# A decoder layer with a 16384-expert lookup on one core: a 4 KB descriptor ring with one more place in five buffers, the h2 copy on VectorE, and outside picks found with bit masks

## The chip, the cores and the metric

The kernel runs on one core of a Trainium2 chip, as one program. TensorE multiplies, VectorE, ScalarE and GpSimd compute, and SP, ScalarE and GpSimd issue transfers. The metric is the device time of one execution in microseconds, as the median of several runs. The profile comes from one more execution, and all its times are counted from the start of its span.

## The reference

One layer works on 512 prompt tokens and 64 sample tokens of width 2048: adaLN modulation, an input projection into a gated linear recurrence and a short convolution, an output projection, a second norm and modulation (its result is called h2), then the expert layer and a last norm. The expert layer is what matters here. For every token and each of 8 heads, two sets of 128 keys are scored, the 16 best of each are combined, and the 16 best of those pairs pick experts out of 128 x 128; an expert is a row `u` of 2048 numbers and a row `v` of 2048.

```python
def peer(h, w_q, sub_keys, expert_u, expert_v):
    ...
        q = (xb @ w_q).reshape(PEER_BLOCK, PEER_HEADS, 2, HALF_DIM)
        sc = jnp.einsum('thpk,pnk->thpn', q, sub_keys).astype(jnp.float32)
        v1, i1 = lax.top_k(sc[:, :, 0], PEER_TOPK)
        v2, i2 = lax.top_k(sc[:, :, 1], PEER_TOPK)
        cand = (v1[..., :, None] + v2[..., None, :]).reshape(PEER_BLOCK, PEER_HEADS, PEER_TOPK * PEER_TOPK)
        cidx = (i1[..., :, None] * N_KEYS + i2[..., None, :]).reshape(PEER_BLOCK, PEER_HEADS, PEER_TOPK * PEER_TOPK)
        top, pos = lax.top_k(cand, PEER_TOPK)
        eidx = jnp.take_along_axis(cidx, pos, axis=-1)
        g = jax.nn.softmax(top, axis=-1).astype(xb.dtype)
        act = jax.nn.gelu(jnp.einsum('td,thkd->thk', xb, expert_u[eidx])) * g
        return jnp.einsum('thk,thkd->td', act, expert_v[eidx])
```

## The kernel before

**The stages.** Phase 1 (to about 1200 us) computes the modulation, the projections, the recurrence, the second norm and the queries. The weights `w_ada` of the modulation are streamed by SP in pieces of 1 MB (`wa`, line 185) into a pool of three buffers, `adap`; the same buffers later carry h2 to memory.

Every matmul of the expert layer is split in three: a float32 operand is rounded on ScalarE (`xhi`, line 904), the rest is taken on GpSimd (`xlo`, line 905), and TensorE adds high times high, high times low and low times high. A raw block travels as `raw` (by SP), then `xhi` and `xlo`, then 24 matmuls. Half a block of 128 experts is the unit `n` of the loop, called a half block here.

**Dense and gathered experts.** The first key of an expert names its block. The 80 blocks that are picked most (L = 80, ranked in `perm`) are computed densely for the 512 prompt tokens: the *U stage* (lines 1373 to 1377) makes the products with all `u` of a block and stores `act`; the *V stage* (line 1393) sums `v` with the weights. What prompt tokens pick from the other 48 blocks, and all picks of the sample tokens, is gathered row by row: GpSimd fetches a row for each of 128 tokens by an indirect transfer of up to 1 MB (line 1203), VectorE multiplies it with the h2 row in PSUM (`dot`, line 1231), and in the second half adds weighted `v` rows up (`add`, line 1258). There are six groups of tokens, the sample tokens and five groups of sorted prompt tokens, with 228 uses of `u` rows and h2 rows and 223 of `v` rows. Each prompt group first fetches its own h2 rows (`fetch_h`) and copies them to PSUM (`use_h`, line 1218).

**Row places.** A row needs one of RB places in the U stage and of RV in the V stage. `gather_to` fetches RB - 1 rows ahead of the use in the U stage, RV - 2 in the V stage.

**Choosing and sorting.** The last head's choice, the softmax and the sort (`choice`, `count`, `sort`) run on VectorE during the first half blocks. `count` marks the outside picks: each of the 512 picks of a partition is compared with each of the 48 outside blocks (lines 1062 to 1064). R1 is the half block in which this generator ends, R2 the one in which `all_slots` ends (the rows of each group are laid out). A generator yields an estimate of VectorE's work in microseconds; the loop adds a fixed credit for each half block (`PIECE`, `PIECE_G`) and goes on with a generator only while credit is left.

**One-hot pairs.** From R1 on, the weight of each dense expert and token is built from one-hot matrices: `g_pair` (line 1559, VectorE) makes two of them for 8 tokens, `g_scale` (line 1567, ScalarE) scales one, `g_mm` (line 1573, TensorE) multiplies them into one PSUM bank, and `g_out` (line 1580, ScalarE) copies that to `stg`. `gm` counts how far each step has come; a pair is scaled one half block after it is made and multiplied LAG half blocks after it is due.

**What sets the order.** In phase 1 a scheduler orders most engines; from the last query head on, each engine runs its instructions in the order of the code. So a late instruction holds all that stands behind it on its engine: an `hT` copy on ScalarE holds `stg`, a row product on VectorE holds `op` and `acc` (line 1415, the sum that frees a PSUM bank for TensorE).

**V stage.** Raw blocks go round four places (two in `ws`, one in `wx`, one in `vx`), loaded seven half-block units ahead (`ahead(n + 7, n + 3)`). Weights (`gsb`, `actr`) are loaded by ScalarE's queue, multiplied (`weigh`, line 1336) and halved (`halve`, lines 1343 and 1347).

Of the kernel before, what the change touches and what calls it, by code (L numbers as in the profile page):

```python
# [5 lines left out]
F32 = mybir.dt.float32  # L6
F32R = mybir.dt.float32r
I32 = mybir.dt.int32
U32 = mybir.dt.uint32
# [28 lines left out]
NCH = NA // TC  # L38
QT = NA // 128
SORTED = ((0, 64, 34), (64, 128, 47), (192, 128, 37), (320, 128, 30), (448, 64, 11))  # L40
RB = 4
RV = 6
ENDS = 5
LATE = 1
PIECE = 5.5
# [2 lines left out]
PIECE_G = 6.9  # L48
HEADS_COUNTED = 4
FULL_ROWS = 1.25  # L50
LAG = 3
FIRST_G = 6
PAIRS = 6
EARLY_V = 16
KEPT = 5
PARTS = 2
# [24 lines left out]
def build(ctx, tc, A, O, dbg=None):  # L81
# [76 lines left out]
    p1 = ExitStack()  # L158
    c1 = p1.enter_context(tc.tile_pool(name="c1", bufs=1))
    big = p1.enter_context(tc.tile_pool(name="big", bufs=1))  # L160
    adap = p1.enter_context(tc.tile_pool(name="adap", bufs=3))
    wk = p1.enter_context(tc.tile_pool(name="wk", bufs=1))
    p1p = ExitStack()
    pp = p1p.enter_context(tc.tile_pool(name="pp", bufs=2, space=PSUM))
# [477 lines left out]
    def pbank(tag, nm, bufs):  # L642
        return psum["p"].tile([128, 512], F32, name=nm, tag=tag, bufs=bufs)
# [236 lines left out]
    def load(n):  # L880
        if n >= len(stream):
            return
        s = stream[n]
        k = n % 3 if n < NU2 + 2 else (n - NU2 - 2) % 4
        pool, b = (ws, 2) if k < 2 else (wx, 1) if k == 2 else (pools["vx"], 1)
        raw = pool.tile([128, 8, 128], F32, name=f"raw{n}", tag="wraw", bufs=b)
        if s[0] == "U":
            nc.sync.dma_start(raw, A["ut"][bass.ds(block(s[1]), 1), :, 8 * s[2]:8 * s[2] + 8, :].rearrange("o p k c -> p (o k) c"))
        else:
            _, i, q = s  # L890
            r2 = raw.rearrange("p (a k) c -> p a (k c)", a=2)
            for a in range(2):
                nc.sync.dma_start(r2[:, a, :], v3[bass.ds(block(i + a), 1), :, q * VC:(q + 1) * VC].rearrange("o p c -> p (o c)"))
        raws[n] = raw
# [159 lines left out]
    def count():  # L1054

        m = nd["m"] = rt.tile([128, 3, QT], F32, name="nd_m")
        fc = rq.tile([128, 2, NA], F32, name="flags", tag="oh", bufs=2)
        fl, code = fc[:, 0, :], fc[:, 1, :]
        i1, i2 = pbank("g", "i1", 2), iselP[:, 1, :]
        S.activation(i1, iselP[:, 0, :], AF.Copy)  # L1060
        yield None
        V.tensor_scalar(fl, i1, perm[:, L:L + 1], None, op0=ALU.is_equal)
        for x in range(L + 1, 128):
            V.scalar_tensor_tensor(fl, i1, perm[:, x:x + 1], fl, op0=ALU.is_equal, op1=ALU.add)
            if x % 8 == 7:
                yield 5.0
        V.scalar_tensor_tensor(code, i1, 128.0, i2, op0=ALU.mult, op1=ALU.add)
        V.scalar_tensor_tensor(code, code, 1.0, fl, op0=ALU.add, op1=ALU.mult)
        V.tensor_reduce(m[:, 0, :], fl.rearrange("p (z k) -> p z k", k=NPK), axis=AX.X, op=ALU.add)
        for z in range(QT):  # L1070
            V.tensor_scalar(m[:, 1, z:z + 1], rowi, float(128 * z), None, op0=ALU.add)
        V.scalar_tensor_tensor(m[:, 2, :], m[:, 0, :], float(NA), m[:, 1, :], op0=ALU.mult, op1=ALU.add)
        yield 5.0
        yield None
        for z in range(QT):
            G.dma_start(pickd[z * 128:(z + 1) * 128, 0:NPK], code[:, z * NPK:(z + 1) * NPK])
            G.dma_start(pickd[z * 128:(z + 1) * 128, NPK:], topv[z].rearrange("p h k -> p (h k)"))
        for _ in range(2):
            yield None
# [126 lines left out]
    def gather_u(i):  # L1206
        p0, n, c = GT[i]
        held, st = {}, {}

        def fetch_h():  # L1210
            held["h"] = new_row(f"h2r{i}")
            G.indirect_dma_start(out=held["h"][0], out_offset=None, in_=h2d,
                                 in_offset=bass.IndirectOffsetOnAxis(ap=tok[:, i:i + 1], axis=0))

        def use_h():
            st["h"] = psum["h"].tile([128, D], F32, name=f"hT{i}", tag="hT", bufs=1)
            r, a = held.pop("h")
            S.activation(st["h"], r, AF.Copy)
            row_log[a] = True

        def fetch(j):
            held[j] = new_row(f"u{i}_{j}")
            take(held[j][0], A["u"], rows_i[i][:, j:j + 1])

        def dot(j):
            if j == 0:
                st.setdefault("h", first_h["h"])
                dots[i] = actp.tile([128, c], F32, name=f"dots{i}", bufs=1)
            r, a = held.pop(j)
            row_log[a] = True  # L1230
            V.scalar_tensor_tensor(r, r, 1.0, st["h"], op0=ALU.mult, op1=ALU.mult, accum_out=dots[i][:, j:j + 1])  # L1231

        if i:
            fetches.append(fetch_h)
            uses.append(use_h)
        for j in range(c):
            fetches.append(lambda j=j: fetch(j))
            uses.append(lambda j=j: dot(j))
# [356 lines left out]
    since = None  # L1595
    spare, due_g = -BEHIND, 0.0
    R1 = R2 = None
    gm = [0, 0, 0, 0]
    ep = None

    def upto(n):
# [9 lines left out]
    for n in range(NU2):  # L1611
# [7 lines left out]
        if R1 is not None:  # L1619
# [8 lines left out]
            while gm[2] < gm[3]:  # L1628
                g_scale(gm[2])
                gm[2] += 1  # L1630
            gm[3] = gm[0]

        even, waits = R2 is not None, False
        while spare > 0 and R2 is None:
# [87 lines left out]
    for m in range(M):  # L1722
        gi, q, bl, first, final = steps[m]
        n = NU2 + 2 * m
        ahead(n + 3, n + 3)
        ahead(n + 7, n + 3)
        if m == last:
            gather_to(NT)
        if m == last + 1:
# [179 lines left out]
```

## Time and profile before

| | |
|---|---|
| median of 3 runs | 3271.31 us (3267.7 to 3271.77) |
| the profiled execution | 3275.15 us |
| its span | 3273.3 us |
| TensorE busy in the span | 3088.6 us, 94% |
| VectorE busy | 2173.3 us, 66% |
| ScalarE busy | 1056.9 us, 32% |
| GpSimd busy | 1718.4 us, 52% |
| mean granted TensorE clock | 0.976 |
| moved by DMA | 882.84 MB, mean 270 GB/s |

Busy shares are means over stages with different limits. Rows of groups read: line, engine, operation, output from inputs, shapes and count, then busy microseconds and mean nanoseconds of one, then the idle time of the engine just before them and what ended it. A wait row reads: who waited, for whom, total microseconds, how often, the longest. In a timeline a row starts with its start and its duration, and the bracket at its end is the idle time before it.

### The profile page before, as it was taken

Reading aid. Unit: us, or ns where it says so; the run is one execution under the profiler, and the core shown is the slowest. Engines: PE = TensorE matmul, PEld = TensorE weight load, DVE = VectorE, ACT = ScalarE, POOL = GpSimd, SP = SyncE. Lnnn points to the kernel's source line nnn. Section 1 sums busy time; section 2 is a strip of 40 time slices with the busy share of each in tenths; the row PEclk is TensorE's granted clock in tenths of the full one; section 3 lists DMA queues with packets and bytes.
Section 4 is the critical chain, followed back from the end, with each engine's and each line's share of the span. In section 5 each row is a group of like instructions: output and inputs, shape, how many; then the busy total and the mean of one; then the engine's idle time right before and its main releaser. Section 6 shows DMA issues by size and latency. Waiting matters only on the chain.

```text
span 3273.3 us, 46692 instructions
## 1 busy us (share of the span) xinstructions
PE 3088.6 (94%) x17239; PEld 2616.8 (80%) x17239; DVE 2173.3 (66%) x3265; ACT 1056.9 (32%) x1645; POOL 1718.4 (52%) x1000
## 2 busy tenths in 40 slices
PE   5999999999989999999999998998999999989897
PEld 2788898889979998887788787886888777777686
DVE  3465521142246898897998979856777787978755
ACT  3244311132232222222665555542222121122122
POOL 2233233344343335666556655656777676777742
PEclk9999999999989999999999999998999999999998
DMA  9744466634342228989779898989999988998964
GB/s 375 266 144 136 163 221 203 214 99 146 131 140 67 72 90 277 308 310 381 312 297 405 340 369 315 395 285 385 389 372 387 391 327 315 344 365 305 369 218 163
DMA packets 297067, 882.84 MB, mean 270 GB/s; under 512 B 37590, under 2 KB 79446, under 8 KB 245366
## 3 DMA queue, kind: packets, MB, share of 16 engines
q1 hardware_dynamic: 160608, 380.39, 33.3%
q0 software_dynamic: 66336, 413.41, 32.1%
q10 hardware_dynamic: 69888, 86.00, 7.5%
q8 instruction: 136, 2.23, 0.3%
q14 instruction: 99, 0.81, 0.1%
HBM read 879.89 MB, written 66.81 MB: 289 GB/s over the span
## 4 chain that ended last, share of the span: by engine, by line
PE 67%; DMA 15%; DVE 7%; issue 4%; POOL 4%; ACT 2%; ACTq 0%; SPq 0%; POOLq 0%; DVEq 0%
PE pu L1373 19%; PE pv L1393 14%; PE pp_o L139 6%; DMA v<-v,rows 4%; DMA gsb<-gd 4%; PE pp_c L139 3%; PE pp_s L139 3%; PE qa L139 3%; PE pp_b L139 3%; PE qb L139 3%; PE gbank L1573 2%; PE pp_x L139 2%; PE pp_y L139 2%; PE ada L189 2%; POOL xlo L905 2%
## 5 line engine op out<-in xcount | busy, mean ns | idle before, releaser
L905 POOL TENSOR_TENSOR xlo<-raw,xhi 128x1024 fp32r<-128x1024 f32 x320 | 785.6, 2467 | 453.8 <-ACT xhi L904 440.5
L904 ACT ACTIVATE xhi<-raw 128x1024 fp32r<-128x1024 f32 x320 | 338.2, 1060 | 868.6 <-PE pv L1393 353.6
L1258 DVE SCALAR_TENSOR_TENSOR accB<-v,dots,accB 128x2048 f32<-128x2048 f32 x211 | 496.3, 2352 | 159.4 <-DMA v<-v,rows 154.0
L1231 DVE SCALAR_TENSOR_TENSOR u<-u,hT 128x2048 f32<-128x2048 f32 x223 | 505.0, 2282 | 145.1 <-DMA u<-u,rows 130.2
L1393 PE MATMUL pv<-ahi,xhi 128*128 128x512 f32 x1280 | 514.8, 402 | 43.7 <-DVE acc L1415 33.7
L1393 PE MATMUL pv<-ahi,xlo 128*128 128x512 f32 x1280 | 510.8, 399 | 10.7 <-POOL xlo L905 10.5
L1373 PE MATMUL pu<-hhi,xhi 128*128 128x512 f32 x1280 | 516.9, 404 | 1.6 <-ACT xhi L904 1.6
L1373 PE MATMUL pu<-hhi,xlo 128*128 128x512 f32 x1280 | 504.7, 394 | 6.5 <-POOL xlo L905 6.5
L1393 PE MATMUL pv<-alo,xhi 128*128 128x512 f32 x1280 | 507.7, 397 | 0.0
L1373 PE MATMUL pu<-hlo,xhi 128*128 128x512 f32 x1280 | 506.0, 395 | 0.0
L1203 POOL DMA_INDIRECT u<-u,rows x223 | 227.6, 1021 | 207.1 <-DVE u L1231 155.2
L1393 PEld LDWEIGHTS pv<-ahi,xhi 128*128 128x128 f32 x1280 | 244.3, 191 | 107.8 <-DVE acc L1415 24.8
L1393 PEld LDWEIGHTS pv<-ahi,xlo 128*128 128x128 f32 x1280 | 244.1, 191 | 72.1 <-POOL xlo L905 15.1
L1203 POOL DMA_INDIRECT v<-v,rows x223 | 260.4, 1168 | 77.9 <-issue 36.3
L1373 PEld LDWEIGHTS pu<-hhi,xlo 128*128 128x128 f32 x1280 | 242.7, 190 | 61.7 <-POOL xlo L905 7.4
L1393 PEld LDWEIGHTS pv<-alo,xhi 128*128 128x128 f32 x1280 | 244.6, 191 | 54.7
L1373 PEld LDWEIGHTS pu<-hhi,xhi 128*128 128x128 f32 x1280 | 243.3, 190 | 52.5 <-ACT xhi L904 2.1
L1373 PEld LDWEIGHTS pu<-hlo,xhi 128*128 128x128 f32 x1280 | 243.0, 190 | 47.8
L1567 ACT ACTIVATE op<-op,it 128x128 f32<-128x128 f32 x512 | 155.9, 389 | 82.5 <-DVE op L1559 82.5
L1573 PEld LDWEIGHTS gbank<-wr,op 128*128 128x128 f32 x1024 | 134.4, 193 | 42.5 <-ACT stg L1580 33.1
L1573 PE MATMUL gbank<-wr,op 128*128 128x80 f32 x1024 | 133.6, 274 | 25.7 <-ACT stg L1580 25.5
L128 POOL TENSOR_TENSOR wlo_q<-raw_q,whi_q 128x1024 fp32r<-128x1024 f32 x28 | 67.8, 2420 | 142.5 <-ACT whi_q L126 142.5
(481 smaller groups left out, 5452.2 us busy)
## 6 DMA issues: line engine op xcount, KB each, us to landing
wa<-w_ada SPq DMA_DIRECT2D x96, 1024.0 KB
raw<-ut SPq DMA_DIRECT2D x160, 512.0 KB
raw<-v SPq DMA_DIRECT2D x320, 256.0 KB
actd<-act ACTq DMA_DIRECT2D x80, 256.0 KB
gd<-stg ACTq DMA_DIRECT2D x64, 320.0 KB
gsb<-gd ACTq DMA_DIRECT2D x80, 256.0 KB
actr<-actd ACTq DMA_DIRECT2D x40, 512.0 KB
raw_o<-w_out SPq DMA_DIRECT2D x32, 512.0 KB
```

The costliest lines, as they stand in the source:

```text
L128: lo_engine(share).tensor_sub(lo, raw, r32(hi))
L139: PE.matmul(o, st, mv[pick](k), start=first, stop=last)
L189: PE.matmul(acc[32 * g:32 * g + 32, :], cpad[:, 4 * kq + g, :], w[:, g, :], start=kq == 0, stop=kq == 3)
L904: S.activation(hi, raw, AF.Copy)
L905: G.tensor_sub(lo, raw, r32(hi))
L1203: G.indirect_dma_start(out=out, out_offset=None, in_=src, in_offset=bass.IndirectOffsetOnAxis(ap=idx, axis=0), bounds_check=NE * 128 - 1, ...
L1231: V.scalar_tensor_tensor(r, r, 1.0, st["h"], op0=ALU.mult, op1=ALU.mult, accum_out=dots[i][:, j:j + 1])
L1258: V.scalar_tensor_tensor(st["a"], r, dots[i][:, j:j + 1], st["a"], op0=ALU.mult, op1=ALU.add)
L1373: PE.matmul(pu, st[:, kk, :], movA[mv](k), start=k == 0 and a == 0, stop=k == KD - 1 and a == 2)
L1393: PE.matmul(pv, st, mv, start=first and j == 0 and a == 0, stop=last and not end and j == SG - 1 and a == 2)
L1567: S.activation(ops[:, j0 + j, :], ops[:, j0 + j, :], AF.Copy, scale=it[2][:, b * 4 + j:b * 4 + j + 1])
L1573: PE.matmul(pg[:, j * L:(j + 1) * L], ops[:, j0 + j, :], wr[:, j0 + j, :], start=True, stop=True)
```

## The change

Six edits go together. The software descriptor ring, an SBUF area in which GpSimd writes the descriptors of its transfers, is set to 4096 bytes for each partition, in place of the default. With the space, five buffers get one more place: rows in the U stage (RB 5) and in the V stage (RV 7), `w_ada` pieces (4), raw V blocks (a fifth place, in `vx`, loaded eight units ahead), and one-hot pairs (PAIRS 8, four buffers in place of three). LAG is 4, and `gm` has a fifth entry, so that a pair is scaled two half blocks after it is made. `use_h` copies the h2 row to PSUM on VectorE. And `count` builds, for each partition, eight words of 16 bits from the 48 outside blocks, selects the word of each pick by eight comparisons, and shifts the pick's bit out of it; it yields 17 us of estimates in place of 30.

```diff
-RB = 4
-RV = 6
+RB = 5
+RV = 7
...
-LAG = 3
+LAG = 4
...
-PAIRS = 6
+PAIRS = 8
...
-    adap = p1.enter_context(tc.tile_pool(name="adap", bufs=3))
+    adap = p1.enter_context(tc.tile_pool(name="adap", bufs=4))
...
-        k = n % 3 if n < NU2 + 2 else (n - NU2 - 2) % 4
-        pool, b = (ws, 2) if k < 2 else (wx, 1) if k == 2 else (pools["vx"], 1)
+        k = n % 3 if n < NU2 + 2 else (n - NU2 - 2) % 5
+        pool, b = (ws, 2) if k < 2 else (wx, 1) if k == 2 else (pools["vx"], 2)
...
+        wb = rq.tile([128, 2, NA], U32, name="words", tag="oh", bufs=2)
+        word, bit = wb[:, 0, :], wb[:, 1, :]
...
+        V.memset(ki[:, 0, :], 1)
+        V.tensor_copy(ki[:, 1, :], perm[:, L:])
+        V.tensor_scalar(ki[:, 2, :], ki[:, 1, :], 15, None, op0=ALU.bitwise_and)
+        V.tensor_tensor(ki[:, 0, :], ki[:, 0, :], ki[:, 2, :], op=ALU.logical_shift_left)
+        V.tensor_scalar(ki[:, 1, :], ki[:, 1, :], 4, None, op0=ALU.logical_shift_right)
+        V.tensor_copy(kf, ki[:, 0:2, :])
+        kt = rq.tile([128, NX_], F32, name="kt", tag="v", bufs=2)
+        for w in range(8):
+            V.scalar_tensor_tensor(kt, kf[:, 1, :], float(w), kf[:, 0, :], op0=ALU.is_equal, op1=ALU.mult,
+                                   accum_out=mk[:, w:w + 1])
+        yield 4.0
         yield None
-        V.tensor_scalar(fl, i1, perm[:, L:L + 1], None, op0=ALU.is_equal)
-        for x in range(L + 1, 128):
-            V.scalar_tensor_tensor(fl, i1, perm[:, x:x + 1], fl, op0=ALU.is_equal, op1=ALU.add)
-            if x % 8 == 7:
-                yield 5.0
+        V.tensor_copy(bit, i1)
+        V.tensor_scalar(word, bit, 4, None, op0=ALU.logical_shift_right)
+        V.tensor_copy(code, word)
+        V.tensor_scalar(bit, bit, 15, None, op0=ALU.bitwise_and)
+        V.tensor_scalar(fl, code, 0.0, mk[:, 0:1], op0=ALU.is_equal, op1=ALU.mult)
+        yield 2.5
+        for w in range(1, 8):
+            V.tensor_scalar(word.bitcast(F32), code, float(w), mk[:, w:w + 1], op0=ALU.is_equal, op1=ALU.mult)
+            V.tensor_add(fl, fl, word.bitcast(F32))
+            if w == 4:
+                yield 4.5
+        V.tensor_copy(word, fl)
+        V.tensor_tensor(word, word, bit, op=ALU.logical_shift_right)
+        V.tensor_scalar(word, word, 1, None, op0=ALU.bitwise_and)
+        V.tensor_copy(fl, word)
+        yield 6.0
...
-            S.activation(st["h"], r, AF.Copy)
+            V.tensor_copy(st["h"], r)
...
-    gm = [0, 0, 0, 0]
+    gm = [0, 0, 0, 0, 0]
...
-            gm[3] = gm[0]
+            gm[3], gm[4] = gm[4], gm[0]
...
-        ahead(n + 7, n + 3)
+        ahead(n + 8, n + 3)
...
-    nc = _bacc.Bacc("TRN2", target_bir_lowering=False, num_devices=1)
+    nc = _bacc.Bacc("TRN2", target_bir_lowering=False, num_devices=1, dynamic_dma_scratch_size=4096)
```

On VectorE, where `count` marks the picks, before (`perm` holds the ranked blocks, `hT` the h2 row in PSUM, `u_27` a gathered row):

```order
L1062 TENSOR_SCALAR flags<-i_12948,perm 128x512
L1064 SCALAR_TENSOR_TENSOR flags<-i_12948,perm,flags 128x512 x15
L1231 SCALAR_TENSOR_TENSOR u_27_12891,dots_11710<-u_27_12891,hT_11373 128x2048
L1231 SCALAR_TENSOR_TENSOR u_28_12950,dots_11710<-u_28_12950,hT_11373 128x2048
L1064 SCALAR_TENSOR_TENSOR flags<-i_12948,perm,flags 128x512 x8
```

The same place with the change (`mk` holds the eight words):

```order
L1075 SCALAR_TENSOR_TENSOR kt,mk<-kf 128x48 x8
L1259 SCALAR_TENSOR_TENSOR u_26_12811,dots_11716<-u_26_12811,hT_11375 128x2048
L1259 SCALAR_TENSOR_TENSOR u_27_12852,dots_11716<-u_27_12852,hT_11375 128x2048
L1079 CAST words<-i_12955 128x512
L1080 TENSOR_SCALAR words<-words 128x512
L1081 CAST flags<-words 128x512
L1082 TENSOR_SCALAR words<-words 128x512
L1083 TENSOR_SCALAR flags<-flags,mk 128x512
L1086 TENSOR_SCALAR words<-flags,mk 128x512
L1087 TENSOR_TENSOR flags<-flags,words 128x512
```

The 48 passes of two inputs between row products have become narrow passes and, for each further word, one comparison and one sum.

On ScalarE in the late U stage, before, at the third h2 copy (`stg` empties the pair bank, `op` is a scaled one-hot matrix):

```order
L1580 ACTIVATE stg_17116<-gbank 128x4x80
L1567 ACTIVATE op_17197<-op_17197,it_13585 128x128 x8
L1218 ACTIVATE hT_17269<-h2r_17206 128x2048
L1580 ACTIVATE stg_17116<-gbank 128x4x80
L1376 ACTIVATE act_17300<-pu_17209 128x512
```

With the change the copy stands on VectorE, at the same group of tokens:

```order
L1259 SCALAR_TENSOR_TENSOR u_46_17006,dots_15646<-u_46_17006,hT_15640 128x2048
L1246 COPY hT_17136<-h2r_17063 128x2048
L1587 TENSOR_TENSOR op_17184<-kb,it_13429 128x1024
L1587 TENSOR_TENSOR wr_17185<-kb,it_13428 128x640
L1259 SCALAR_TENSOR_TENSOR u_0_17066,dots_17192<-u_0_17066,hT_17136 128x2048
```

The copy has moved from in front of a `stg` on ScalarE to in front of a pair on VectorE, behind the last product that reads the old row.

On ScalarE at the first scaled pair, before and then with the change (both begin at the copy of `iota` to `kb`, in whose half block the pairs begin; the first pair is made one half block later):

```order
L1547 ACTIVATE kb<-iota 128x128
L904 ACTIVATE xhi_14240<-raw_14150 128x1024
L1376 ACTIVATE act_14280<-pu_14210 128x512
L1377 DMA actd<-act_14280 128x512
L904 ACTIVATE xhi_14288<-raw_14235 128x1024
L1567 ACTIVATE op_14244<-op_14244,it_13585 128x128 x8
```

```order
L1575 ACTIVATE kb<-iota 128x128
L904 ACTIVATE xhi_14085<-raw_13995 128x1024
L1404 ACTIVATE act_14127<-pu_14055 128x512
L1405 DMA actd<-act_14127 128x512
L904 ACTIVATE xhi_14135<-raw_14080 128x1024
L904 ACTIVATE xhi_14181<-raw_14130 128x1024
L1595 ACTIVATE op_14089<-op_14089,it_13430 128x128 x8
```

One more `xhi`, that is one more half block, lies between the making of a pair and its scaling.

More of the change, by code (lines that the diff above doesn't have):

```diff
@@ L1058, in count @@
         fl, code = fc[:, 0, :], fc[:, 1, :]
+        wb = rq.tile([128, 2, NA], U32, name="words", tag="oh", bufs=2)
+        word, bit = wb[:, 0, :], wb[:, 1, :]
         i1, i2 = pbank("g", "i1", 2), iselP[:, 1, :]
         S.activation(i1, iselP[:, 0, :], AF.Copy)
-        yield None
-        V.tensor_scalar(fl, i1, perm[:, L:L + 1], None, op0=ALU.is_equal)
-        for x in range(L + 1, 128):
-            V.scalar_tensor_tensor(fl, i1, perm[:, x:x + 1], fl, op0=ALU.is_equal, op1=ALU.add)
-            if x % 8 == 7:
-                yield 5.0
+        NX_ = 128 - L
+        ki = rq.tile([128, 3, NX_], U32, name="ki", tag="v", bufs=2)
+        kf = rq.tile([128, 2, NX_], F32, name="kf", tag="cand", bufs=2)
+        mk = rt.tile([128, 8], F32, name="mk")
+        V.memset(ki[:, 0, :], 1)
[9 more added lines that the diff above has]
+        yield 4.0
+        yield None
+        V.tensor_copy(bit, i1)
[14 more added lines that the diff above has]
+        yield 6.0
         V.scalar_tensor_tensor(code, i1, 128.0, i2, op0=ALU.mult, op1=ALU.add)
```

## The prediction

> **What bounds the kernel now.** I read the stage table first (one row per stretch; after the stretch's length come each engine's busy microseconds with its instructions, then the granted TensorE clock, the DMA share and GB/s).
>
> ```profile
> 0.00:120.00 120.00, 81.57 (x532) 42.80 (x532) 42.12 (x99) 35.22 (x57) 33.67 (x34) 0.93 1.02 379
> 120.00:920.00 800.00, 787.19 (x5844) 723.72 (x5848) 293.13 (x449) 234.38 (x309) 286.47 (x123) 0.99 0.47 160
> 920.00:950.00 30.00, 19.09 (x125) 13.36 (x118) 21.53 (x40) 12.02 (x22) 13.41 (x10) 0.77 0.38 133
> ...
> 1200.00:1540.00 340.00, 339.32 (x1520) 275.19 (x1519) 281.46 (x497) 98.28 (x127) 217.86 (x130) 1.00 0.84 299
> 1540.00:2263.00 723.00, 689.17 (x3455) 577.38 (x3454) 599.36 (x789) 382.64 (x797) 430.46 (x287) 0.98 0.89 346
> 2263.00:2560.00 297.00, 288.08 (x1236) 233.01 (x1235) 220.25 (x123) 77.75 (x78) 206.09 (x120) 0.98 1.00 380
> 2560.00:3115.00 555.00, 509.58 (x2115) 404.29 (x2114) 444.83 (x254) 113.58 (x103) 391.21 (x235) 0.97 0.92 342
> ```
>
> The first 120 us belong to the DMA engines (share 1.02). From there to the end TensorE is the bound, and what can be won is its idle time and the clock that it loses after idling. Before 1540 us there is little: 0.7 us idle from 1200 on. The losses that this change can touch lie in the late U stage (1540 to 2263, where one-hot pairs are made beside the U blocks) and in the middle of the V stage (2560 to 3115). Second came the waits of TensorE: the first three lines below are from 1540 to 2263, the next three from 2560 to 3115, the last from 920 to 950 (total, times, longest).
>
> ```profile
> PE gbank L1573 <- ACT stg L1580: 25.5, 15, 5.6
> PE pu L1373 <- POOL xlo L905: 6.5, 2, 4.8
> PE pu L1373 <- ACT xhi L904: 1.6, 1, 1.6
> ...
> PE pv L1393 <- DVE acc L1415: 33.7, 18, 4.9
> PE pv L1393 <- POOL xlo L905: 9.3, 6, 3.0
> PE pv L1393 <- ACT xhi L904: 2.3, 1, 2.3
> ...
> PE pm L199 <- ACT part L192: 7.0, 1, 7.0
> ```
>
> So the waits are 33.6 us in the late U stage and 45.3 us in the middle of V. The clock adds its own part: 723 us at 0.98 lose (1 - 0.98) x 723 = 14.5 us, 555 us at 0.97 lose 16.7 us. **Recoverable at most: 48 us and 62 us.** Third, who is behind ScalarE and VectorE in these stretches (the first three lines from 1540 to 2263, the last two from 2560 to 3115):
>
> ```profile
> DVE u L1231 <- DMA u<-u,rows: 81.3, 59, 4.7
> ...
> DVE u L1231 <- ACT stg L1580: 12.1, 2, 11.6
> ...
> ACT op L1567 <- DVE op L1559: 82.5, 37, 11.5
> ...
> DVE accB L1258 <- DMA v<-v,rows: 84.5, 42, 10.0
> ...
> ACT xhi L904 <- DMA raw<-v: 122.8, 27, 21.2
> ```
>
> Both chains begin at a gathered row that lands late. VectorE waits for it, what is queued behind it on VectorE (`op`, `acc`) comes late, then ScalarE's `stg`, then TensorE.
>
> **The change part by part.**
>
> *The h2 copy.* The timeline at 1888 us shows ScalarE at its hT copy and then TensorE at the matmul that waited, the last two lines the next such copy and its matmul:
>
> ```profile
> 1887.97 1.88 ACT L1218 ACTIVATE hT<-h2r 128x2048 f32<-128x2048 f32 x1 [5.35 <-DVE u L1231]
> 1889.78 0.69 ACT L1580 ACTIVATE stg<-gbank 128x320 f32<-128x320 f32 x1
> ...
> 1890.52 1.99 PE L1573 MATMUL gbank<-wr,op 128*128 128x80 f32 x8 [4.49 <-ACT stg L1580]
> ...
> 2034.38 1.88 ACT L1218 ACTIVATE hT<-h2r 128x2048 f32<-128x2048 f32 x1 [6.76 <-DVE u L1231]
> ...
> 2037.90 2.00 PE L1573 MATMUL gbank<-wr,op 128*128 128x80 f32 x8 [5.55 <-ACT stg L1580]
> ```
>
> ScalarE stood 5.35 us in front of hT, because VectorE still multiplied with the old one, and `stg`, queued behind, held TensorE 4.49 us. At 2034 us it stood 6.76 us and TensorE 5.55 us, the longest wait of its list. On VectorE the copy needs no wait for another compute engine: those two waits, 10.0 us, go. What is late next is the h2 row's own gather, and the copy is VectorE work. The nearest row is a pass over the same shape into PSUM, 2.35 us; the removed ScalarE form is 1.88 us:
>
> ```profile
> L1255 DVE TENSOR_SCALAR accB<-v,dots x6: 2353/2353/2355, 2206.8 to 3015.4; 128x2048 f32<-128x2048 f32 x6
> ...
> L1218 ACT ACTIVATE hT<-h2r x5: 1881/1883/1988, 1581.2 to 2151.9; 128x2048 f32<-128x2048 f32 x5
> ```
>
> Five copies are 11.8 us on VectorE, in exchange for its 12.1 us of waiting; queued behind each are `op` and the row products, as behind any late row. Bounds on the path: 10.0 us gained, 11.8 us lost. I take the gain, since VectorE has 723 - 599 = 124 us free there.
>
> *LAG 4, eight pairs, scaling one step later.* ScalarE's 82.5 us before `op` come from asking for the scaling one half block after VectorE was asked for the pair. Now it is two.
>
> ```profile
> L1573 PE MATMUL gbank<-wr,op 128*128 128x80 f32 x1024 | 133.6, 274 | 25.7 <-ACT stg L1580 25.5
> ...
> 1559.99 2.45 ACT L1567 ACTIVATE op<-op,it 128x128 f32<-128x128 f32 x8 [11.52 <-DVE op L1559]
> 1562.34 1.04 ACT L904 ACTIVATE xhi<-raw 128x1024 fp32r<-128x1024 f32 x1
> ```
>
> Without the 1024 of the pairs, 3455 - 1024 = 2431 matmuls at 24 a half block are 101 half blocks in 723 us, 7.1 us each. So ScalarE's waits below 7 us would disappear, and the one of 11.5 us, behind which xhi and then xlo came late and cost TensorE 4.8 us, shrinks to 4.4. What is late next is VectorE itself, not helped by this edit: it must still make every pair. The remaining 33.6 - 10.0 = 23.5 us could go wholly or not at all; I take half, 12 us, because VectorE's 81 us of row waits also feed `wr` and `op` and only the fifth place helps there.
>
> *Fifth and seventh row place.* A row is asked for one use earlier in both stages. In the middle of V, 139 uses (131 + 4 + 4) fall in 555 us, 4.0 us apart; VectorE's 42 waits average 2.0 us:
>
> ```profile
> L1258 DVE SCALAR_TENSOR_TENSOR accB<-v,dots,accB 128x2048 f32<-128x2048 f32 x131 | 308.1, 2352 | 88.9 <-DMA v<-v,rows 84.5 <-issue 2.8
> ```
>
> If rows landed as soon after their issue as now, nearly all of TensorE's 45.3 us would go. They won't: all loads share the DMA engines, at 0.92 in this stretch and at 1.00 (380 GB/s) in the one before, and the moved bytes, 342 x 555 = 190 MB, need 500 us at 380. Bounds 0 and 62; I take a third, 21 us, clock included. The fifth raw place and the load eight half blocks ahead belong to the same answer: they bring raw blocks earlier from the same DMA engines, and SP meets the same waits in the same order. The Trainium skill, page "DMA: Bandwidth & Descriptors", section "Issuing engines are not separate DMA queues", says that all transfers run on the same 16 engines and interleave. Read strictly, more transfers in flight would add no bandwidth and the V term would be 0; the trace bears this out between 2263 and 2560 and leaves 8% open from 2560 on.
>
> *Bit masks.* This removes one and 47 passes, and adds 11 + 4 passes with one source, 8 with two, and 14 narrow ones:
>
> ```profile
> L1064 DVE SCALAR_TENSOR_TENSOR flags<-i,perm,flags 128x512 f32<-128x512 f32 x47 | 35.3, 751 | 1.5
> ...
> L1100 DVE TENSOR_SCALAR ohs<-io,rk x4: 485/486/486, 1495.2 to 1498.7; 128x512 f32<-128x512 f32 x4
> ```
>
> Removed 35.3 + 0.5 us; added 15 x 0.49 + 8 x 0.75 + 14 x (at most 0.49) = 7.4 + 6 + 6.9 = 20 us at most. VectorE gains 15 us or more around 1400 us, where TensorE idles 0.7 us in 340: no direct gain. Indirectly the sort ends four half blocks sooner (57 to 53 by the planner's own costs), so pairs begin earlier and spread over 87 half blocks instead of 83. I book 0, with bounds of a few us either way.
>
> *Fourth w_ada buffer.* In the first 120 us the DMA engines are full: 0. At 930 us the last load lands earlier and `part` moves ahead of two `hhi` steps on ScalarE; the modulation behind it sets the pace next. Of 7.0 us I take 2, bounds 0 and 7. A fifth row's clearing adds one GpSimd pass, 1.8 us, beside matmuls that idle little there:
>
> ```profile
> L840 POOL MEMSET row<- x4: 1803/1810/1812, 958.9 to 964.2; 128x2048 f32 x4
> ```
>
> *Ring.* A gather costs GpSimd about a microsecond now:
>
> ```profile
> L1203 POOL DMA_INDIRECT v<-v,rows x206: 987/998/3089, 2274.0 to 3113.3; - x103
> ```
>
> That is 0.998 us at the median; no row shows a short ring. Below, GpSimd can't gain; above, it would wait for older transfers. I take 0, since at most five gathers are outstanding. The skill's page "SBUF — State Buffer", section "SBUF size: 192, 224, or 256?", gives 16 KiB for this ring, and the section "The descriptor swizzle" of the DMA page 9 descriptors an engine for a 1 MiB transfer; with 16 bytes each (its "Terms"), 4 KB hold an estimated 28 such gathers. By that the ring costs nothing, and the trace has no case against it.
>
> **Sum.** Late U: 10.0 + 12 = 22 us of waits, and of the clock's 14.5 us the same part (22/33.6), 9.5 us: 32 us. Middle of V: 21. Fourth buffer: 2. Together 55 us off the profiled 3275.2 us: 3220. That execution lies 3.8 us above the median of the runs, 3271.3, so the forecast is **3216 us**.
>
> **The rivals.**
> 1. *The DMA engines are full, and depth buys nothing in V.* For it: share 1.00 at 380 GB/s before 2560. Against it: 0.92 and 342 GB/s where TensorE waits. Only U and the buffer remain: 3271 - 34 = 3237.
> 2. *All waits are jitter, and one more place absorbs them.* U 48, V 62, `pm` 2: 3271 - 112 = 3159. For it: the V waits of VectorE average half of a row's interval. Against it: VectorE would be busy 599 + 12 in 675 us, 90%, in bursts.
> 3. *VectorE becomes the bound.* Its 11.8 us of copies land on the path, the 10.0 us of hT waits go with their clock (10.0/33.6 of 14.5 is 4.4), and row waits eat the rest: 3271 + 11.8 - 10.0 - 4.4 = 3269, no change that shows. This is also the case in which the change does not do what it says. For it: 599 of 723 us busy already. Against it: 81 us of the remainder are row waits, which the fifth place shortens.
> 4. *Slower: GpSimd waits for ring space.* In the middle of V it is busy 391 of 555 us, so 139 gathers can each grow by 164/139 = 1.2 us before it fills up and `xlo`, queued behind, holds TensorE. At 1.6 us more per gather it is 0.4 x 139 = 56 us over: about 3327. For it: gathers and `xlo` share one queue. Against it: no wait of that kind in the trace.
>
> **How the numbers follow.** Forecast 0.51, rivals 0.22, 0.12, 0.08 and 0.07. A change under 0.2% (6.5 us), about what a measurement of this kernel tells from none, is "same". Faster: 0.51 + 0.22 + 0.12 = 0.85; same 0.08; slower 0.07. The range goes from 3165, which leaves out the end of rival 2, to 3262, short of rivals 3 and 4. It takes in the forecast with its open bounds: no U gain beyond hT and no V gain is 3271 - 10 = 3261.
>
> **What would show it.** hT copies on VectorE near 2.35 us, and no wait above 4 us of `gbank` for `stg`; ScalarE's 82.5 us before `op` down by more than half; TensorE's waits for `acc` near 25 us with the DMA share above 0.92 between 2560 and the end of V; gathers still at 1.0 us. Wrong it would be if `acc` waits grow, if waits for `xlo` replace those for `stg`, or if GpSimd's gathers lengthen.

## The result, and the profile after

The changed kernel takes **3231.77 us** (median of 4 runs, 3228.94 to 3246.16) where the kernel before takes 3271.54 us beside it: ratio 0.9879, 95% interval 0.9852 to 0.9905, 40 us less. The forecast was 3216 us, its range 3165 to 3262. The profiled execution went from a span of 3273.3 to 3231.5 us, 41.8 us less.

Where these 41.8 us lie is read from the first and the last matmul of the two dense stages. The view is that of one source line (count, duration in ns as min/median/max, first and last start in us). Before, U and V:

```profile
L1373 PE MATMUL pu<-hhi,xhi x1280: 387/393/774, 1200.5 to 2261.8; 128*128 128x512 f32 x183
...
L1393 PE MATMUL pv<-ahi,xhi x1280: 387/393/793, 2262.5 to 3247.3; 128*128 128x512 f32 x183
```

And after:

```profile
L1401 PE MATMUL pu<-hhi,xhi x1280: 387/392/774, 1194.4 to 2221.0; 128*128 128x512 f32 x183
...
L1421 PE MATMUL pv<-ahi,xhi x1280: 387/393/796, 2221.7 to 3206.3; 128*128 128x512 f32 x183
```

| stretch | before, us | after, us | difference | forecast |
|---|---|---|---|---|
| start to the first U matmul | 1200.5 | 1194.4 | -6.1 | -2 |
| U: to the first V matmul | 1062.0 | 1027.3 | **-34.7** | -32 |
| V: first to last matmul | 984.8 | 984.6 | **-0.2** | -21 |
| rest | 26.0 | 25.2 | -0.8 | 0 |

U came out close to the forecast, and V won nothing that shows. The stage table of the changed kernel (columns as in the one of before) is cut at about the same places of the work: its first row ends at the first U matmul, late U ends at the first V matmul, and the last two rows are given the lengths that they have before, 297 and 555 us.

```profile
0.00:1194.40 1194.40, 1127.41 (x8256) 1013.47 (x8257) 546.88 (x1511) 346.95 (x494) 420.61 (x205) 0.98 0.47 167
...
1534.00:2221.70 687.70, 678.99 (x3443) 571.49 (x3443) 590.38 (x741) 367.73 (x777) 427.58 (x285) 0.99 0.91 359
2221.70:2519.00 297.30, 290.59 (x1248) 235.59 (x1247) 223.71 (x127) 78.81 (x79) 209.81 (x123) 0.98 1.00 385
2519.00:3074.00 555.00, 505.95 (x2104) 403.20 (x2103) 447.98 (x249) 112.03 (x103) 385.69 (x231) 0.96 0.90 338
```

Late U now needs 687.7 us with TensorE idle 8.7 (34 before), at 0.99. In the middle of V nothing is better: in the same 555 us TensorE is busy 506 us instead of 510 and makes 2104 matmuls instead of 2115, and the DMA engines are busy 0.90 instead of 0.92. What TensorE waits for, the first line from late U, the other three from 2221.7 to 3074 (total, times, longest):

```profile
PE gbank L1601 <- ACT stg L1608: 8.7, 8, 3.5
...
PE pv L1421 <- DVE acc L1443: 33.7, 13, 5.9
PE pv L1421 <- ACT xhi L904: 13.1, 3, 5.5
PE pv L1421 <- POOL xlo L905: 8.8, 6, 2.7
```

In U, 25.5 us behind `stg` became 8.7, with no wait over 3.5 us, and those for `xlo` and `xhi` (8.1 us) are gone. In V the three make 55.6 us. In the same stretch of before (2262.5 to 3115) they made 53.9:

```profile
PE pv L1393 <- DVE acc L1415: 33.7, 18, 4.9
PE pv L1393 <- POOL xlo L905: 10.5, 7, 3.0
PE pv L1393 <- ACT xhi L904: 9.7, 2, 7.4
```

VectorE tells more. Its waits in that stretch of before:

```profile
DVE accB L1258 <- DMA v<-v,rows: 134.2, 64, 10.0
DVE actr L1336 <- DMA raw<-v: 13.3, 3, 7.3
DVE acc L1415 <- PE pv L1393: 12.1, 8, 2.9
DVE actr L1336 <- DMA actr<-actd: 9.5, 3, 4.3
```

and after:

```profile
DVE accB L1286 <- DMA v<-v,rows: 53.3, 32, 5.4
DVE acc L1443 <- PE pv L1421: 47.6, 24, 5.9
DVE actr L1364 <- DMA raw<-v: 46.4, 6, 13.3
DVE actr L1364 <- DMA actr<-actd: 26.9, 3, 10.3
```

The rows are late far less (134 us down to 53). But `actr`, the weighting of the loaded activations (`weigh`), now waits 73.3 us for its loads instead of 22.8. The four lines sum to 169 us before and to 174 after; since VectorE does the same passes in stretches of the same length, such a sum has to stay, and what it says is only that the waits changed their names. Further, in late U ScalarE's 82.5 us before `op` are now 28.2, and VectorE's 81.3 us for `u` rows are 63.9:

```profile
ACT op L1595 <- DVE op L1587: 28.2, 22, 4.9
...
DVE u L1259 <- DMA u<-u,rows: 63.9, 43, 5.1
```

The h2 copies and the gathers of the changed kernel:

```profile
L1246 DVE COPY hT<-h2r x5: 2282/2286/2295, 1561.1 to 2099.8; 128x2048 f32<-128x2048 f32 x5
...
L1231 POOL DMA_INDIRECT u<-u,rows x223: 986/999/1807, 1230.4 to 2144.1; - x112
L1231 POOL DMA_INDIRECT v<-v,rows x223: 986/996/3104, 2149.5 to 3072.8; - x112
```

2.29 us a copy, and gathers at 1.0 us, as forecast.

### The profile page after: what moved, and what is told of

Read it like the earlier page. It is cut to its first block, busy times and chain, and to the rows that moved or that the text cites. A ratio compares the mean times of both kernels' runs of the same rounds, so it can differ in the third digit from the quotient of the medians.

```text
span 3231.5 us, 46649 instructions
## 1 busy us (share of the span) xinstructions
PE 3078.4 (95%) x17239; PEld 2612.9 (81%) x17239; DVE 2174.3 (67%) x3267; ACT 1045.7 (32%) x1640; POOL 1712.5 (53%) x1001
## 4 chain that ended last, share of the span: by engine, by line
PE 70%; DMA 13%; DVE 6%; issue 5%; POOL 5%; ACT 1%; SPq 0%; ACTq 0%; POOLq 0%; DVEq 0%
PE pu L1401 19%; PE pv L1421 16%; PE pp_o L139 6%; DMA gsb<-gd 4%; PE pp_c L139 3%; PE pp_s L139 3%; DMA actr<-actd 3%; PE qa L139 3%; PE pp_b L139 3%; PE qb L139 3%; PE ada L189 3%; PE pp_x L139 2%; PE pp_y L139 2%; DMA v<-v,rows 2%; POOL xlo L905 2%
## 5 line engine op out<-in xcount | busy, mean ns | idle before, releaser
L1421 PE MATMUL pv<-ahi,xhi 128*128 128x512 f32 x1280 | 514.7, 402 | 46.8 <-DVE acc L1443 33.7
L1601 PEld LDWEIGHTS gbank<-wr,op 128*128 128x128 f32 x1024 | 133.8, 192 | 22.4 <-ACT stg L1608 12.9
L1443 DVE TENSOR_TENSOR acc<-acc,pv 128x512 f32<-128x512 f32 x144 | 96.5, 680 | 72.6 <-PE pv L1421 72.3
L128 POOL TENSOR_TENSOR wlo_o<-raw_o,whi_o 128x1024 fp32r<-128x1024 f32 x32 | 77.6, 2424 | 119.9 <-ACT whi_o L126 119.9
## 6 DMA issues: line engine op xcount, KB each, us to landing
actr<-actd ACTq DMA_DIRECT2D x40, 512.0 KB, 15.5
```

The lines of the kernel that those rows point to most:

```text
L1421: PE.matmul(pv, st, mv, start=first and j == 0 and a == 0, stop=last and not end and j == SG - 1 and a == 2)
L1443: V.tensor_add(ak, ak, pv)
L1601: PE.matmul(pg[:, j * L:(j + 1) * L], ops[:, j0 + j, :], wr[:, j0 + j, :], start=True, stop=True)
```

## The experiments

My theory after the result: U won by the h2 copy, the longer lag and the fifth row place together; V won nothing because VectorE, having its rows, now waits in order for the loads of `weigh`. The rival for V: the DMA engines carry all that they can, so that whatever is asked for earlier pushes something else back. The table has the kernel before, the changed kernel and twelve further ones, with their measured ratio to before, and U and V as in the table above (from one profiled execution each). The kernel with half v rows leaves out half of each gathered `v` row; it is a test and not a version to keep.

| kernel | ratio | 95% interval | U, us | V, us |
|---|---|---|---|---|
| before | 1 | | 1062.0 | 984.8 |
| changed | 0.9879 | 0.9852 to 0.9905 | 1027.3 | 984.6 |
| changed, h2 copy on ScalarE | 0.9948 | 0.9928 to 0.9967 | 1056.5 | 979.4 |
| changed, LAG 3 and six pairs | 0.9910 | 0.9889 to 0.9931 | 1039.5 | 990.5 |
| changed, 4 and 6 row places | 0.9917 | 0.9894 to 0.9941 | 1051.4 | 974.8 |
| changed, 47 passes for the flags | 0.9894 | 0.9872 to 0.9916 | 1026.1 | 1002.8 |
| changed, three w_ada buffers | 0.9874 | 0.9855 to 0.9892 | 1028.3 | 989.4 |
| changed, four raw places in V | 0.9867 | 0.9848 to 0.9887 | 1032.3 | 990.2 |
| before, h2 copy on VectorE | 0.9960 | 0.9948 to 0.9973 | 1050.5 | 987.9 |
| before, ring of 4 KB | 0.9979 | 0.9963 to 0.9995 | 1061.6 | 975.6 |
| changed, weigh later | 0.9818 | 0.9795 to 0.9841 | 1036.0 | 979.4 |
| changed, half v rows | 0.9642 | 0.9626 to 0.9658 | 1025.5 | 908.0 |
| changed, alo in two passes | 0.9881 | 0.9864 to 0.9899 | 1028.6 | 975.6 |
| changed, weigh later and alo in two | 0.9831 | 0.9814 to 0.9848 | 1032.0 | 967.4 |

V swings between executions. Three kernels have its code as before and give 975.6 to 987.9 us; five have it as changed, with edits elsewhere, and give 979.4 to 1002.8. The means are 982.8 and 989.3, so nothing of the 21 us shows. U repeats within 0.4 us in the two kernels that have its code as before, 1062.0 and 1061.6; but in the six further kernels that have it as changed, with edits before or behind it, it runs from 1025.5 to 1036.0. So one profile tells U to about ten microseconds and V to about twenty.

**The h2 copy, undone.**

```diff
-            V.tensor_copy(st["h"], r)
+            S.activation(st["h"], r, AF.Copy)
```

> The changed kernel with the copy of the h2 rows to PSUM back on ScalarE, all else as changed (3231.8 us). In the changed kernel the late U stage lost 34 us against before. My theory gives 10 us of waits and 4 us of clock to this copy: about 3246 us, with gbank waits for stg above 4 us again and the U stage 10 to 14 us longer than the 1027.5 us of the changed kernel. The rival, that the longer lag had covered ScalarE's wait anyway, gives 3232 us and an unchanged U stage; a third, that the copies cost VectorE their 11.8 us, gives under 3225 us.

Ratio 0.9948: 0.69% of the time comes back, 23 us, and 29 us of U. The direction is that of my theory, the size one and a half times to twice as large. The timeline of this kernel at 1867 us shows the longest wait:

```profile
1867.27 1.88 ACT L1246 ACTIVATE hT<-h2r 128x2048 f32<-128x2048 f32 x1 [12.65 <-DVE u L1259]
...
1869.09 0.71 ACT L1608 ACTIVATE stg<-gbank 128x320 f32<-128x320 f32 x1
...
1869.85 1.57 PE L1601 MATMUL gbank<-wr,op 128*128 128x80 f32 x6 [13.16 <-ACT stg L1608]
```

ScalarE stands 12.65 us before the copy until VectorE has multiplied the last row with the old h2 row, and TensorE stands 13.16 us behind it. My reading is that with five row places and the longer lag ScalarE comes to the copy earlier while VectorE does not; its waits for `op` are 12.9 us here. No run tests that reading alone.

**The h2 copy, alone.** The same edit the other way round in the kernel before.

> The kernel before with the h2 copy on VectorE as its only change. The prediction's term: 10.0 us of waits and 4.4 us of clock less: about 3257 us, ratio 0.9955. Undoing it in the changed kernel cost 0.69% (22 us), so a second theory, that a wait for stg behind the copy is worth more than itself (xhi and xlo queue behind it too): ratio 0.992 to 0.994. The rival, that VectorE's 11.8 us of copies eat the gain and it pays only beside the longer lag: ratio 0.998 to 1.002.

Ratio 0.996, 13 us, and 11.5 us of U: about what the prediction booked, 14.4. The waits of TensorE for `stg` in late U (1541 to 2252.4) fall by 7.7 us from 25.5, and the two long ones behind the copy are gone:

```profile
PE gbank L1573 <- ACT stg L1580: 17.8, 11, 3.7
PE pu L1373 <- POOL xlo L905: 6.6, 2, 4.9
```

**Lag and pairs, undone.**

```diff
-LAG = 4
+LAG = 3
-PAIRS = 8
+PAIRS = 6
-    gm = [0, 0, 0, 0, 0]
+    gm = [0, 0, 0, 0]
-            gm[3], gm[4] = gm[4], gm[0]
+            gm[3] = gm[0]
```

> The changed kernel with LAG 3, six pairs and the scaling one half block after the pair again. My theory: ScalarE's waits for op on VectorE, 26.4 us in the late U stage of the changed kernel, go back to about 80, and TensorE loses 10 to 17 us in the U stage: 3242 to 3249 us. The rival, that the fifth row place or the h2 copy alone did it: 3232 us, U stage within 3 us of 1027.5.

Ratio 0.991, 10 us, and 12 us of U, as the theory said, but not clear of the noise: the interval overlaps that of the changed kernel, and 1039.5 lies 3.5 us above the range in which U runs with its code as changed. What shows clearly is the step behind it. ScalarE's waits for `op` rose from 28.2 to 61.2 us, where the seven further kernels with this code as changed have 26.6 to 36.5. They did not rise to 80; that the rest of the change keeps VectorE somewhat ahead is my reading.

**Row places, undone.**

```diff
-RB = 5
-RV = 7
+RB = 4
+RV = 6
```

> The changed kernel with four and six row places again instead of five and seven. In the V stage nothing was won (985.7 us before, 985.4 after), although VectorE's waits for v rows fell from 84.5 to 35.0 us in its middle. My theory, that VectorE only waits elsewhere now (for the act load before weigh, and stretched alo): V stays within 4 us of 985.4, VectorE's row waits go back to about 85, and U gets 0 to 6 us longer: 3232 to 3238 us. The rival, that the places do win in V and something else of the change lost the same there: V gets 10 to 20 us longer, over 3242 us.

A miss on U, which I had at 0 to 6 us and which got 24 us longer, 15 us above its range; right on V, which did not get longer without the places (974.8). The total is 0.9917, 12 us back, and its interval overlaps that of the changed kernel. ScalarE's waits for `op` rise to 51.5 us. VectorE's waits for rows in V go back to 114.5 us, and those for the loads of `weigh` fall to 30.6. In late U (1537 to 2248.4) TensorE waits behind late blocks again:

```profile
PE gbank L1601 <- ACT stg L1608: 10.4, 11, 2.9
PE pu L1401 <- POOL xlo L905: 9.0, 3, 7.5
```

Undone one at a time, the three cost U 29, 12 and 24 us, together 65, while all of U's gain is 34.7. In the whole time they cost 23, 10 and 12 us, together 45, and the whole gain is 40. So the profiles hint that they overlap, each one missing leaving ScalarE or VectorE late in the same places, but the times, with intervals of several microseconds each, don't show it.

**Bit masks, undone.**

```diff
...
+        V.tensor_scalar(fl, i1, perm[:, L:L + 1], None, op0=ALU.is_equal)
+        for x in range(L + 1, 128):
+            V.scalar_tensor_tensor(fl, i1, perm[:, x:x + 1], fl, op0=ALU.is_equal, op1=ALU.add)
...
```

> The changed kernel with the 47 passes over the outside picks instead of the bit masks. Prediction and theory: no direct cost, since TensorE idles under 1 us there; the sort ends four half blocks later, so the pairs crowd into 83 instead of 87 half blocks: 0 to 5 us, 3232 to 3237 us. The rival, that the earlier sort carries the late U gain: 10 us or more, over 3242 us, with the added waits of TensorE near the end of the U stage.

Ratio 0.9894, its interval overlaps that of the changed kernel, and U is 1026.1 against 1027.3. The pairs begin 24 us later without the masks (at 1548.5 instead of 1524.3 us), so the earlier sort is there, but it buys nothing that shows. V is longer in this profile, where nothing was edited.

**Three w_ada buffers.**

```diff
-    adap = p1.enter_context(tc.tile_pool(name="adap", bufs=4))
+    adap = p1.enter_context(tc.tile_pool(name="adap", bufs=3))
```

> The changed kernel with three w_ada buffers. The prediction gave the fourth buffer 2 us; the profiles show U beginning at 1194.4 us in the changed kernel and at 1200.5 before. If the buffer does it, U begins near 1200 again and the time is 4 to 6 us longer (ratio 0.989 to 0.990); if that was chance between executions, U begins at 1193 to 1197 and the ratio stays at 0.988.

Inconclusive in the time (0.9874), clear in the traces: U begins at 1202.8 us, and TensorE waits 38.7 us for w_ada loads in the first 1200. Before it was 36.4, in the changed kernel 29.0, from the same view of these three, first this kernel, then before, then the changed one. The other runs bear it out: U begins at 1200.5 to 1202.8 us in the four kernels with three buffers and at 1193.1 to 1200.9 in the ten with four, in the mean at 1201.5 and 1196.2.

```profile
PE ada L189 <- DMA wa<-w_ada: 38.7, 15, 18.6
PE pm L199 <- ACT part L192: 7.2, 1, 7.2
```

```profile
PE ada L189 <- DMA wa<-w_ada: 36.4, 15, 18.2
```

```profile
PE ada L189 <- DMA wa<-w_ada: 29.0, 9, 18.9
...
PE pm L199 <- ACT part L192: 4.3, 1, 4.3
```

**The ring, alone.**

```diff
-    nc = _bacc.Bacc("TRN2", target_bir_lowering=False, num_devices=1)
+    nc = _bacc.Bacc("TRN2", target_bir_lowering=False, num_devices=1, dynamic_dma_scratch_size=4096)
```

> The kernel before with the descriptor ring of 4 KB as its only change. The prediction: nothing, ratio 0.998 to 1.002, gathers at 1.0 us at the median. The rival, ring space: gathers of 1.5 us or more at the median in V, waits for xlo, ratio above 1.005.

Ratio 0.9979, gathers at 0.998 us at the median and 3.103 at the most, as before. The smaller ring costs nothing that shows. The interval lies just below 1 by 0.05%; I draw nothing from that.

**Four raw places in V.**

```diff
-        k = n % 3 if n < NU2 + 2 else (n - NU2 - 2) % 5
-        pool, b = (ws, 2) if k < 2 else (wx, 1) if k == 2 else (pools["vx"], 2)
+        k = n % 3 if n < NU2 + 2 else (n - NU2 - 2) % 4
+        pool, b = (ws, 2) if k < 2 else (wx, 1) if k == 2 else (pools["vx"], 1)
...
-        ahead(n + 8, n + 3)
+        ahead(n + 7, n + 3)
```

> The changed kernel with four raw places in V and loads seven half blocks ahead, as before. If deeper loading of raw blocks is what pushes the act loads back (VectorE waits 73 us for weigh's loads in the changed kernel, 23 before), these waits fall below 45 and V gets a few us shorter or stays (ratio 0.985 to 0.988). If the deeper loading helps TensorE, its waits for xhi and xlo in V (21.9 us) grow by 5 or more and the ratio rises to 0.990 or above.

VectorE's waits for the loads of `weigh` fall from 73.3 to 26.0 us, TensorE's for `xhi` and `xlo` do not grow (15.7), and the ratio is 0.9867. So the deeper loading of raw blocks brings V nothing that shows. But neither is V shorter (990.2): the wait goes elsewhere once more, to `acc` (VectorE waits 68.9 us there for TensorE). That deeper raw loads alone delay the activation loads is not shown: these waits are 61 to 73 us in the six kernels that have both more row places and more raw places and ask for `weigh` as before, and they fall as far, to 30.6 us, when the row places are undone and the raw places stay.

**weigh later.** Its loads stay where they are.

```diff
-        jobs.setdefault(h_ - 4, []).append(lambda sg=sg: weigh(sg))
+        jobs.setdefault(h_ - 2, []).append(lambda sg=sg: weigh(sg))
```

> The changed kernel with weigh (the product of acts and weights of four blocks) asked for two columns, 5.5 us, later on VectorE in the V stage; its loads stay where they are. In the changed kernel VectorE waits 73 us in order for these loads (46.4 + 26.9, at most 13.3) and row products, acc behind it come late. My theory, that this wait took the place of the row waits and holds TensorE: the 73 us fall below 40, TensorE's 55.6 us of waits in V fall by 10 to 25, V takes 960 to 975 us instead of 985: ratio to before 0.981 to 0.985. The rival, that the DMA engines are simply full: the waits move once more (to rows, xhi or acc on TensorE), V stays within 5 us of 985, ratio 0.986 to 0.990.

The time says my theory, 0.9818. The profile, taken of an execution of 3236 us where the median is 3222, says the rival: waits for weigh's loads fall to 31.5 us, but those for rows rise to 88.8, and TensorE still waits 53.2 us. Taken alone, the profile settles nothing about the cause; in the time, 20 us are won over the changed kernel at the same bytes, and the intervals of the two do not meet.

**Half v rows.** This one separates VectorE from the DMA engines.

```diff
...
-            take(held[j][0], A["v"], rows_i[i][:, j:j + 1])
...
+            take(held[j][0][:, 0:D // 2], A["v"].rearrange("r (h c) -> (r h) c", h=2), rows_i[i][:, j:j + 1])
...
-                V.scalar_tensor_tensor(st["a"], r, dots[i][:, j:j + 1], st["a"], op0=ALU.mult, op1=ALU.add)
+                V.scalar_tensor_tensor(two(st["a"]), twice(r), dots[i][:, j:j + 1], two(st["a"]), op0=ALU.mult, op1=ALU.add)
...
```

`two` views a row as two halves, and `twice` gives the first half of a row two times.

> The changed kernel with half of each gathered v row left out (4 KB of the table for each token instead of 8; the last row of each group is whole), while VectorE's passes keep their size by reading that half twice. It takes about 0.5 MB x 200 = 100 MB off the DMA engines in V and nothing off VectorE. If the DMA engines are what bounds V's waits, VectorE's waits for rows and weigh's loads vanish nearly and V falls to 945 to 960 us (985 less the 56 us of waits, part of the clock beside it): ratio near 0.978. If VectorE's own order is the cause (acc queued behind several row products and alo), TensorE's waits for acc stay above 20 us and V stays above 970.

V falls to 908.0 us, by more than either theory had. TensorE has not one wait for `acc`, `xhi` or `xlo` in V; it is busy in all but 2.7 us of the two stretches shown (these 2.7 us go to `tok`, a load of the last steps), and the clock is at 1.00:

```profile
2226.40:2524.00 297.60, 297.60 (x1292) 242.39 (x1291) 229.29 (x128) 77.14 (x79) 220.60 (x128) 1.00 0.83 282
2524.00:3079.00 555.00, 552.26 (x2414) 450.01 (x2412) 465.01 (x282) 130.88 (x120) 405.51 (x242) 1.00 0.75 256
```

VectorE does the same passes, even more of them in 555 us (465 us busy). It isn't the bound of V, and the order in which it takes them costs TensorE nothing as long as the loads come in time. The page's list of DMA issues shows what changed (KB each, median us to landing); of the changed kernel:

```profile
raw<-v SPq DMA_DIRECT2D x320, 256.0 KB, 7.9
...
actr<-actd ACTq DMA_DIRECT2D x40, 512.0 KB, 15.5
```

and with half rows:

```profile
raw<-v SPq DMA_DIRECT2D x320, 256.0 KB, 4.2
...
actr<-actd ACTq DMA_DIRECT2D x40, 512.0 KB, 5.5
```

And the sums that the transfer view gives for the 852 us from V's first matmul on, before, changed, and with half rows (whose 852 us hold some 350 matmuls more):

```profile
DMA packets 114268, 302.79 MB, mean 355 GB/s; under 512 B 13437, under 2 KB 50267, under 8 KB 90934
```

```profile
DMA packets 114621, 302.28 MB, mean 355 GB/s; under 512 B 13541, under 2 KB 50361, under 8 KB 91458
```

```profile
DMA packets 122227, 226.26 MB, mean 265 GB/s; under 512 B 16419, under 2 KB 53283, under 8 KB 120508
```

Before and after move the same bytes at the same 355 GB/s, with one row place more, one raw place more and a load asked for earlier. That rate by itself shows no ceiling: the same bytes in the same time give the same rate. Half rows show more. What holds TensorE in V is loads that land late, and they land in time when a quarter of the bytes is gone. So much of the rival holds. That the engines can carry no more does not follow: in the first 297 us of V they are the fullest (share 1.00, 385 GB/s) and TensorE idles 6.7 us, while in the next 555 us, at 0.90 and 338 GB/s, it idles 49.

**alo in two passes**, the second one column later.

```diff
...
-        V.tensor_sub(lo, acts.pop(sg), r32(hi))
+        i = slice((part - 1) * SG // 2, part * SG // 2)
+        V.tensor_sub(lo[:, i, :], acts[sg][:, i, :], r32(hi[:, i, :]))
...
         jobs.setdefault(h_ + 2, []).append(lambda sg=sg: halve(sg, 1))
+        jobs.setdefault(h_ + 3, []).append(lambda sg=sg: halve(sg, 2))
```

> The changed kernel with alo (one pass of 128x2048, 3.4 to 6.5 us on VectorE) made as two passes of 128x1024, the second one column (2.8 us) later, so that acc can pass between. Several of TensorE's longest waits for acc in V (6.1 us at 2909, 6.1 at 3008) end right behind such a pass. If that pass is the price, these waits shrink by some 3 us each and V gets 10 to 20 us shorter (ratio 0.982 to 0.985); if it is only the last of several things that are late together, V stays within 5 us (ratio 0.986 to 0.990).

Ratio 0.9881: no gain that shows. The longest wait for `acc` shrank from 5.9 to 4.1 us, but there are 17 instead of 13. The edit had less to win than expected: in the changed kernel eleven of the 20 passes took 2.29 us or less.

**Both.**

> The changed kernel with both: weigh two columns later and alo in two passes. With half rows every wait of V vanished, so the DMA engines stand behind V's waits, and these two edits only make VectorE wait less in order for what lands late. If they add up: later weigh alone gave 0.9818, alo alone 0.9881, both near 0.981, V about 970 to 978 us, with VectorE's waits for weigh's loads below 40 us (73 in the changed kernel). If the engine time that is saved comes back as waits for rows and raw blocks, ratio 0.985 to 0.989 and TensorE's waits in V stay above 50 us.

Ratio 0.9831, interval 0.9814 to 0.9848, which lies below the changed kernel's whole interval, as that of later `weigh` alone does: a version faster than before and than the changed kernel, 3220 us where the kernel before takes 3274.8 beside it. Weigh's loads hold VectorE 37.7 us (73.3 in the changed kernel). TensorE's waits from 2220 to 3072:

```profile
PE pv L1425 <- DVE acc L1447: 21.3, 11, 3.9
PE pv L1425 <- POOL xlo L905: 11.4, 10, 1.9
PE pv L1425 <- ACT xhi L904: 8.4, 5, 2.3
```

That is 41.1 us against 55.6, and V of 967.4 us. Later `weigh` alone has the same time within the intervals, so that the split of `alo` adds nothing that shows.

## Why the prediction was right, and where it was wrong

**Late U, -32: right, -34.7.** *The h2 copy* was booked at 14.4 us (10.0 of waits, 4.4 of clock) and measured 13 us alone; no wait for `stg` over 4 us is left; a copy takes 2.29 us, not 2.35. *Lag, pairs and the fifth place* were to bring "half" of the other 23.5 us and their clock, 17 us; with 34.7 - 11.5 = 23 us they brought more, if the copy is counted as it measures alone. The prediction put these 17 us down to the lag and gave the fifth place no price in U. Undone, the place costs U 24 us and the lag 12; the whole times, 12 and 10 us, don't tell the two apart. So the place had a share that the prediction left out, and its size stays open.

**Middle of V, -21: wrong, -0.2.** This is the step that failed: "I take a third". The prediction saw that all loads share the DMA engines, and took the 8% that they had free in the mean for room that more places could use. The places did what they were to do for the rows, and it did not reach TensorE: VectorE's waits moved from rows (134 to 53 us) to the loads of `weigh` (23 to 73) and to waits for TensorE before `acc` (12 to 48), and TensorE waits 55.6 us instead of 53.9. Undoing the row places or the raw place leaves V where it was (974.8 and 990.2 us). With a quarter of the bytes gone all of TensorE's waits on these engines went, 77 us of V with their clock, though VectorE's work was the same. The page "DMA: Bandwidth & Descriptors" of the Trainium skill, section "Issuing engines are not separate DMA queues", has transfers from all engines interleave on the same 16. The prediction's own strict reading of it made the V term 0, and the trace agrees with that: -0.2 us.

**Fourth w_ada buffer, -2: too small, -6.1** in the profile. Over all kernels the means with three and with four buffers differ by 5 us. The prediction put nothing into the first 120 us since the DMA engines are full there. But TensorE's waits for these loads fell from 36.4 to 29.0 us, 5.9 us of that in the first 120, besides 2.7 us of `pm`; with three buffers they are 38.7. That this shows in the whole time is not settled: the kernel with three buffers measures 0.9874.

**Bit masks 0 and ring 0: right**, within 0.2% or so each. The passes that the masks add were to take 20 us at most and take 22.5: three of the passes over 512 elements with one source took 2.5 us each, the others 0.41 to 0.68.

**The rivals.** That the DMA engines are full and depth buys nothing in V (given 0.22, 3237 us) is what V did; its time lies 5 us from the measured one, the forecast 16. That VectorE becomes the bound in U, with 3269 us, fell with the h2 copy alone, which won 13 us; for V half rows show the same. That GpSimd waits for ring space fell with the ring alone. The forecast's 55 us came out as 42 in the profile: U and the buffer brought 7 us more than booked, which made up for a third of what V did not bring. That they did was luck, and no part of the working. Of the signs named, the DMA share above 0.92 and `acc` waits near 25 us did not come: 0.90 and 33.7. What stays open is how much of V's waiting is bytes and how much is their bunching, since half rows take away both. Later `weigh` won 20 us over the changed kernel, and with the split `alo` 16, at the same bytes; so the order of the work still has a part in it.

## What to carry to other kernels

Before a deeper prefetch is given a gain, list the other loads that the same DMA engines carry in the stretch, and ask which of them will land late instead: here, at 355 GB/s in the mean and 385 in the fullest stretch, a place more only changed which load is late, and VectorE's waits (169 and 174 us) changed their names. A cheap test tells late loads from an engine that is too slow: halve the bytes and keep the passes. It does not tell bytes from bunching. And where several edits cure one chain of waits, undo them one by one from the full change as well as trying one alone: the h2 copy was worth 11.5 us of U alone and 29 as the missing part (13 and 23 us of the time, where the intervals still meet).

## What had not been expected of the hardware

Loads took much longer to land at a higher DMA share: an activation load of 512 KB took 5.5 us at the median where V ran at a share of 0.75 to 0.83, and 15.5 us at 0.90 to 1.00; a raw block 4.2 and 7.9 us. The 15.5 us are the upper end, for the other kernels with whole rows whose pages list this time have 9.1 to 13.7. A mean idle share of eight per cent was no reserve here. And the pass `alo` (128x2048, two sources) took between 2.28 and 7.19 us in the changed kernel, eleven times 2.29 us or less and six times over 5.5, all six behind 2600 us, where TensorE waits too:

```profile
L1375 DVE TENSOR_TENSOR alo<-actr,ahi x20: 2281/2286/7186, 2199.6 to 3094.0; 128x2048 fp32r<-128x2048 f32 x20
```

That it is GpSimd's `xlo` which stretches it fits their times (4.67 us for two `xlo` at 2901.24 beside an `alo` of 6.33 from 2901.74), but no run was made to show it.
